# Loading the first two tiles of a row-maximum kernel side by side, from two queues, at the first instruction

## The chip, the cores and the metric

The kernel runs on one core of one Trainium2 chip. The metric is the device time of one execution in microseconds (us), lower is better. The profile's own span is some 1.8 us shorter than the device time (626.4 us of the 628.2 us of the profiled run before), so spans are compared with spans and times with times.

## The reference

```python
def reference(x):                                  # x: 8192 x 8192 float32
    return np.linalg.norm(x, ord=np.inf, axis=1)   # per row: the largest |x|
```

All 268.4 MB have to be read once; the result is 32 KB.

## The kernel before

Three quarters of the rows are the bulk: 24 tiles of 128 partitions x 16384 values, two rows in each partition, 64 KB per partition and 8.39 MB per tile. SyncE's queue loads them into three rotating buffers, and VectorE takes the absolute maximum of each row. The last quarter is cut into ever smaller loads, so that little is left to do after the last byte.

```python
    sbuf = ctx.enter_context(tc.tile_pool(name="sbuf", bufs=BUFS))    # BUFS = 3
    ...
    for a in range(A):                    # A = 6
        for n in range(G):                # G = 4
            t = sbuf.tile([P, W + PAD], F32, tag="t")
            nc.sync.dma_start(out=t[:, :W], in_=x_b[a, n])
            absmax(
                r_bulk[:, a, n * B : (n + 1) * B],
                t[:, :W].rearrange("p (b c) -> p b c", b=B),
            )
    nc.scalar.dma_start(out=out_b, in_=r_bulk[:])
    # ... the last quarter: smaller loads, all from SyncE's queue ...
    nc.at_finalize(start_first_load_early)
    nc.at_finalize(finish_on_pool)
```

`start_first_load_early` is already a start-up optimisation: it moves SyncE's first load ahead of everything else in SyncE's program, so that it is issued before the barrier with which the engines begin.

## Time and profile before

| | before |
|---|---|
| time, median of 3 runs | 628.01 us (627.74 to 628.76) |
| span of the profiled run | 626.4 us |
| the 16 DMA engines | full from 1 us on, 433 GB/s in the steady part |
| VectorE | busy 552.9 us, 88% |
| one tile | transfer 19.35 us, reduce 17.22 us |

The table says that the transfer is the bound: a reduce is 2.1 us shorter than a transfer, so VectorE waits for each tile, and a microsecond that the DMA engines lose is a microsecond of the result. I call a "round" what the 16 DMA engines do in 2.42 us, namely one 64 KB packet each (a packet is the piece of a load that one engine moves at a time). A bulk tile is 8 rounds.

### The profile page before, as it was taken

The page shows a single profiled execution, that of the slowest core. Times are in us where ns is not written, and L with a number is a line of the kernel's source. Part 1 is how long each engine was busy: PE and PEld are TensorE (multiplying, and loading weights), DVE is VectorE, ACT ScalarE, POOL GpSimd, SP SyncE. Part 2 cuts the span into 40 slices and gives each one's busy share as a digit, 9 for nine tenths or more (in the row PEclk, how much of TensorE's full clock was granted, in tenths as well). Part 3 has the DMA queues.
Part 4 walks back from the last instruction along what each step waited for, and adds up shares of the span by engine and source line. Part 5 has one row for each costly group of instructions (what it writes and reads, how often), then busy time and mean ns, then how long its engine had stood idle before and what let it go on. Part 6 is the DMA issues. An engine that isn't in the chain of part 4 may idle for free.

```text
span 626.4 us, 204 instructions
## 1 busy us (share of the span) xinstructions
DVE 552.9 (88%) x67; POOL 0.2 (0%) x4
## 2 busy tenths in 40 slices
DVE  0588988889988889888898888988889999999998
POOL 0000000000000000000000000000000000000000
DMA  9999999999999999999999999999999999999997
GB/s 402 469 402 452 418 452 418 448 423 402 469 402 469 402 469 402 469 402 469 402 469 402 465 406 452 418 452 418 452 404 426 438 428 425 439 423 431 426 422 311
DMA packets 9282, 268.49 MB, mean 429 GB/s; under 512 B 1856, under 2 KB 1856, under 8 KB 3392
## 3 DMA queue, kind: packets, MB, share of 16 engines
q1 hardware_dynamic: 8496, 268.45, 99.4%
q10 hardware_dynamic: 784, 0.02, 0.1%
q14 instruction: 2, 0.02, 0.0%
HBM read 268.44 MB, written 0.03 MB: 429 GB/s over the span
## 4 chain that ended last, share of the span: by engine, by line
DMA 63%; DVE 35%; issue 1%; another core or an unknown queue 0%; DVEq 0%
DMA t<-in_x_dram 63%; DVE r_bulk L140 24%; DVE part L140 8%; DVE t L140 3%; DVEq L220 0%; DVE r_tail L140 0%
## 5 line engine op out<-in xcount | busy, mean ns | idle before, releaser
L140 DVE TENSOR_REDUCE r_bulk<-t 128x2 f32<-128x16384 f32 x24 | 413.3, 17220 | 70.0 <-DMA t<-in_x_dram 70.0
L140 DVE TENSOR_REDUCE part<-t 128x1 f32<-128x8192 f32 (+20 forms) x28 | 121.6, 4410 | 0.9 <-DMA t<-in_x_dram 0.8
L140 DVE TENSOR_REDUCE t<-t 128x1 f32<-128x1664 f32 (+8 forms) x11 | 16.5, 1572 | 0.0
L140 DVE TENSOR_REDUCE r_tail<-t 128x1 f32<-128x644 f32 (+1 forms) x2 | 1.5, 814 | 0.0
L137 DVE MEMSET part<- 128x56 f32 x1 | 0.1, 105 | 0.9 <-PEq L209 0.9
L140 DVE TENSOR_REDUCE r_tail<-part 128x14 f32<-128x56 f32 x1 | 0.2, 211 | 0.0
L209 POOL MEMSET const-bfloat16-1.0<- 128x1 bf16 x1 | 0.1, 101 | 0.0
L209 POOL MEMSET const-uint8-127<- 128x1 uint8 x1 | 0.1, 101 | 0.0
L209 POOL MEMSET const-float32-0.0<- 128x1 f32 x1 | 0.1, 98 | 0.2 <-issue 0.2
L209 POOL MEMSET const-float32-1.0<- 128x1 f32 x1 | 0.1, 98 | 0.0
## 6 DMA issues: line engine op xcount, KB each, us to landing
t<-in_x_dram SPq DMA_DIRECT2D x2, 3392.0 KB, 37.3
t<-in_x_dram SPq DMA_DIRECT2D x1, 5376.0 KB, 40.6
t<-in_x_dram SPq DMA_DIRECT2D x1, 4864.0 KB, 32.9
t<-in_x_dram SPq DMA_DIRECT2D x1, 4800.0 KB, 33.0
t<-in_x_dram SPq DMA_DIRECT2D x1, 4672.0 KB, 34.9
t<-in_x_dram SPq DMA_DIRECT2D x3, 1536.0 KB, 28.7
t<-in_x_dram SPq DMA_DIRECT2D x1, 3520.0 KB, 42.9
t<-in_x_dram SPq DMA_DIRECT2D x1, 3328.0 KB, 40.4
```

What stands on the lines that cost most here:

```text
L137: nc.vector.memset(part[:], 0.0)
L140: nc.vector.reduce_max(out=o, in_=i, axis=X, apply_absolute_value=True)
L209: nc = _bacc.Bacc("TRN2", target_bir_lowering=False, num_devices=1)
```

## The change

The intent is to have the second tile's load in flight from the start too, on a queue of its own. Tile 2's load goes to ScalarE's queue, and both first loads are moved to the head of their engines' programs.

```diff
-def start_first_load_early(nc):
-    sp = mybir.EngineType.SP
+def start_first_loads_early(nc):
     first, *rest = nc.main_func.blocks
-    for block in rest:
-        ...                # the first DMA of SP, moved to the head of the program
+    for engine in (mybir.EngineType.SP, mybir.EngineType.Activation):
+        block, load = next(
+            (b, i)
+            for b in rest
+            for i in b.instructions
+            if i.engine == engine and type(i).__name__ == "InstDMACopy"
+        )
+        assert not load.sync_info.on_wait
+        ...                # moved to the head of that engine's program
@@
-            nc.sync.dma_start(out=t[:, :W], in_=x_b[a, n])
+            queue = nc.scalar if a * G + n == 1 else nc.sync
+            queue.dma_start(out=t[:, :W], in_=x_b[a, n])
```

More of the change, by code (lines that the diff above doesn't have):

```diff
@@ L45, in segments @@
     return out
-def start_first_load_early(nc):
-    sp = mybir.EngineType.SP
+def start_first_loads_early(nc):
     first, *rest = nc.main_func.blocks
-    for block in rest:
-        insts = block.instructions
-        for i, ins in enumerate(insts):
-            if ins.engine == sp and type(ins).__name__ == "InstDMACopy":
-                assert not ins.sync_info.on_wait
-                moved = insts[i]
-                block.instructions = insts[:i] + insts[i + 1 :]
-                head = first.instructions
-                at = next(k for k, h in enumerate(head) if h.engine == sp)
-                first.instructions = head[:at] + [moved] + head[at:]
-                return
+    for engine in (mybir.EngineType.SP, mybir.EngineType.Activation):
[6 more added lines that the diff above has]
+        assert not load.sync_info.on_wait
+        block.instructions = [i for i in block.instructions if i.name != load.name]
+        head = first.instructions
+        at = next(k for k, h in enumerate(head) if h.engine == engine)
+        first.instructions = head[:at] + [load] + head[at:]
 def finish_on_pool(nc):
@@ L192 @@
     nc.sync.dma_start(out=out_t, in_=r_tail[:])
-    nc.at_finalize(start_first_load_early)
+    nc.at_finalize(start_first_loads_early)
     nc.at_finalize(finish_on_pool)
```

## The prediction

> **What bounds the kernel now.** I read the page first, then windows over the first microseconds, then the order of time, then the store at the end of the bulk part. The change only concerns the start, so the question is whether any DMA time is lost there. These are whole lines of the page: the busy tenths in 40 slices, the load queue, and the costliest group.
>
> ```profile
> DVE  0588988889988889888898888988889999999998
> ...
> DMA  9999999999999999999999999999999999999997
> ...
> q1 hardware_dynamic: 8496, 268.45, 99.4%
> ...
> L140 DVE TENSOR_REDUCE r_bulk<-t 128x2 f32<-128x16384 f32 x24 | 413.3, 17220 | 70.0 <-DMA t<-in_x_dram 70.0
> ```
>
> The DMA engines are full in every slice but the last; packets of the one load queue fill 99.4% of the 16 engines' time. VectorE is idle only ahead of the 24 bulk reduces, 70.0 us in all, and always because of a load. The bound is the transfer of 268.4 MB. Windows of the start, and one long window of the steady part (length, busy times, clock, DMA share, GB/s):
>
> ```profile
> 0.00:0.90 0.90, 0.03 (x1) 0.20 (x4) 1.00 0.00 0
> 0.90:1.70 0.80, 0.07 (x1) 0.00 (x0) 1.00 3.80 1311
> 1.70:3.80 2.10, 0.00 (x0) 0.00 (x0) 1.00 0.00 0
> 3.80:4.80 1.00, 0.00 (x0) 0.00 (x0) 1.00 2.42 1049
> ...
> 100.00:400.00 300.00, 267.96 (x16) 0.00 (x0) 1.00 1.00 433
> ```
>
> A packet is booked whole in the window in which it starts. 0.80 us x 1311 GB/s is 1.05 MB, which is 16 packets of 64 KB, one for each engine: the first round of packets starts between 0.9 and 1.7 us, so the load issued at 0.0 needs about 1.0 us to its first byte. The next round starts between 3.8 and 4.8 us, some 3.0 us after the first. In the steady part a round of 1.05 MB takes 1.0486 MB / 433 GB/s = 2.42 us. So the start costs 1.0 us of empty engines and 0.6 us of a slow first round; I see nothing else lost. A tile of 8.39 MB is 8 rounds, 19.35 us. The order of time:
>
> ```profile
> 0.00 58.80 SPq L145 DMA_DIRECT2D t<-in_x_dram  x5
> ...
> 21.95 17.22 DVE L140 TENSOR_REDUCE r_bulk<-t 128x2 f32<-128x16384 f32 x1 [20.98 <-DMA t<-in_x_dram]
> 41.22 17.22 DVE L140 TENSOR_REDUCE r_bulk<-t 128x2 f32<-128x16384 f32 x1 [2.05 <-DMA t<-in_x_dram]
> 60.59 17.22 DVE L140 TENSOR_REDUCE r_bulk<-t 128x2 f32<-128x16384 f32 x1 [2.14 <-DMA t<-in_x_dram]
> ```
>
> Tiles land at about 21.9, 41.2 and 60.6 us, 19.3 us apart: one tile's transfer time with no gap. Between 0 and 2 us the same view counts three load issues on SyncE's queue (at 0.00, 0.79 and 1.17 us), so the second load waits in the queue from about 1 us on, and its turn comes only some 20 us later. Issuing it 0.8 us sooner brings nothing by itself.
>
> **What the Trainium skill says.** "DMA: Bandwidth & Descriptors", section "Issuing engines are not separate DMA queues": transfers started by different engines end on the same 16 DMA engines and interleave, and several issuers only save the sequencers' issue time. Section "Queues, rings and completion order" of that page: each DMA engine goes round between the queues that have work, packet by packet. The trace of before agrees with both, because one transfer of it, the bulk result's store, comes from ScalarE's queue while loads run (the page's lines, then the DMA view of the window 487.8 to 543):
>
> ```profile
> q10 hardware_dynamic: 784, 0.02, 0.1%
> ...
> out_dram<-r_bulk ACTq DMA_DIRECT2D x1, 24.0 KB, 59.1
> ```
> ```profile
> DMA packets 1580, 24.00 MB, mean 435 GB/s; under 512 B 864, under 2 KB 864, under 8 KB 864
> ...
> q1 hardware_dynamic: 796, 23.97, 100.5%
> q10 hardware_dynamic: 784, 0.02, 0.8%
> ```
>
> A store of 24 KB took 59.1 us, since its 784 packets went one for one with 796 load packets. And the rate during this alternation is 435 GB/s against 433 alone: changing queues costs nothing that shows. The page's section "Where 436 GB/s comes from" puts the ceiling of the 16 ports at 435 GB/s; the measured 433 is already there, so a second queue has no idle bandwidth to take. "Perfetto Trace Analysis", section "DMA Instruction — HWDGE (DVE, Sync)", says that an issuing sequencer locks the descriptor generator for itself; no run here shows yet two issues at once, but if it holds the second issue waits some 0.4 us (an issue lasts 0.33 to 0.61 us here), not more.
>
> **The change part by part.** It removes one SyncE issue (0.33 us, not on the path: the engines have 20 us of work by then). It adds one issue on ScalarE, which does nothing else until 484 us. ScalarE and SyncE then reach the opening barrier perhaps 0.4 us later; this delays VectorE's small memset and the third load's issue (now at about 1.2 us), neither of which is needed before 20 us. Cost on the path: 0.
>
> What does move is the order of bytes. Tile 1 (SyncE) and tile 2 (ScalarE) now alternate. With strict turns tile 1 gets the odd rounds, 1 to 15, and tile 2 the even ones, 2 to 16; tile 3, behind tile 1 in SyncE's queue, gets 17 to 24. Tile 1 lands 7 rounds later than now, 21.95 + 7 x 2.42 = 38.9 us; tile 2 at 41.2 and tile 3 at 60.6 us as now. The first reduce starts at 38.9 instead of 21.95 us, so VectorE is 17 us late. (The alternation may start later: the store was issued at 484.2 us, and all its packets lie after 487.8, so a queue that is ahead may keep its lead for a few packets. With four rounds of lead tile 1 lands on round 12, at 31.6 us; tile 3 then starts to take turns with the rest of tile 2, which lands on round 19, at 48.6 us. VectorE is then late by a similar amount.)
>
> Does the lateness reach the loads? A load waits for the reduce that frees its buffer (three buffers). With one reduce each 17.24 us from 38.9, reduces end and the next loads are issued at 56.1 (load 4), 73.4 (load 5) and 90.6 us (load 6), instead of 39.2, 58.5 and 77.8. The engines need them when the load before is through: at about 60, 79.9 and 99.3 us. The slack is 4, 6.5 and 8.7 us, growing by 19.35 - 17.24 = 2.1 us per tile, and a fresh issue needs 1.0 us to its first byte. So the queue never runs dry. VectorE makes up 17 us at 2.1 us per tile within about 8 tiles; from about 180 us on, everything is where it was. Its total agrees: 38.9 + 24 x 17.24 = 452.7 us, less than the 467 us at which the last bulk reduce starts now.
>
> The end is then untouched: the last loads land near 623 us as now, followed by the same short reduce and store. Sum: 0 on the start, 0 in the rate, 0 at the end, so 628.0 us.
>
> **The rivals.**
> First, a gain: two queues could fill part of the 1.0 us before the first byte or the slow first round. For it: that is the only empty DMA time in the trace. Against it: the first load is already the first instruction, ScalarE starts no sooner, and one packet per engine is enough to keep the engine occupied. The most it can give is 1.0 + 0.6 = 1.6 us, 626.4 us; I expect at most a few tenths.
>
> Second, VectorE's lateness becomes a new wait. If both tiles end together at 41.2 us (for instance if ScalarE's packets go first, since the reduces run in program order), load 4 is issued at 58.5 and has its first byte at 59.5 us, when the first engines have just run out. A bubble of up to 1 us would then stay to the end, since the DMA bound never gives time back: 629 us. For it: the slack there is about nothing. Against it: SyncE's issue comes first in the trace by some 0.1 us, and later loads have several us.
>
> Third, large packets from two queues might not interleave freely: if each change of queue cost what the first round did, 15 changes x 0.6 us would be 9 us, 637 us. Against it: 435 GB/s in the store's window, though the store's packets are tiny. Even this is within 2%.
>
> Fourth, there is no alternation of 64 KB packets at all, and tile 1 goes wholly first: then the trace stays as it is, 628.0 us.
>
> **Range and chances.** The main line and the fourth rival give 628.0; the first pulls down to 626.4 at most, the second up to 629. Runs of the kernel before alone spread from 627.74 to 628.76. I choose 628.0 with 626.9 to 629.1. Two per cent is 12.6 us, and no mechanism above reaches it: faster 0.01, within 2% 0.98, slower 0.01.
>
> **What would show each step right or wrong.** Right: VectorE's first reduce starts between 31 and 41 us and its idle time before it nearly doubles; the next eight or so reduces run with no idle time between them; total idle before the bulk reduces stays near 70 us; the window 100 to 400 us shows 433 GB/s; loads 4 to 6 are issued some 17 us later; the page's DMA line stays at 9 in all slices. If the first reduce stays at 22 us, the fourth rival holds. A window between 56 and 64 us under 433 GB/s would be the second rival's bubble; a lower rate between 1 and 41 us the third. The prediction is wrong if the first round starts clearly before 0.9 us, if two queues together exceed 433 GB/s, or if loads are issued late beyond the first three.

## The result

| | before | after |
|---|---|---|
| time, median of 6 runs | 627.96 us (627.74 to 628.76) | 631.16 us (630.74 to 631.53) |
| span of the profiled run | 626.4 us | 629.5 us |
| ratio | 1 | 1.0049, 95% interval 1.0036 to 1.0062 |

Ratios here are the mean time of one kernel's fast runs over that of the other's of the same rounds, so they are not quite the ratio of the medians quoted. The change costs 3.2 us. That is half a per cent, but well outside the scatter. The page of the changed kernel, the same lines as before plus the second queue's:

```profile
DVE  0039999999988898888998888988889999999998
...
DMA  9999999999999999999999999999999999999996
...
q1 hardware_dynamic: 8352, 260.06, 96.0%
q10 hardware_dynamic: 928, 8.41, 3.2%
...
L140 DVE TENSOR_REDUCE r_bulk<-t 128x2 f32<-128x16384 f32 x24 | 412.6, 17217 | 74.1 <-DMA t<-in_x_dram 74.1
```

VectorE now starts in the third slice of 15.7 us rather than the second, then works without idle slices, and is back in step by slice 12. Its total idle time ahead of the bulk reduces went from 70.0 to 74.1 us, so it is not slower; something it waits for came later. At 40 slices the DMA line hides what happened. The order of time shows the start (start, length, engine, what; in brackets the idle time before and its end):

```profile
0.00 198.19 SPq L147 DMA_DIRECT2D t<-in_x_dram  x11
0.12 0.39 ACTq L147 DMA_DIRECT2D t<-in_x_dram  x1
...
41.90 137.10 DVE L140 TENSOR_REDUCE r_bulk<-t 128x2 f32<-128x16384 f32 x8 [40.78 <-DMA t<-in_x_dram]
180.61 17.22 DVE L140 TENSOR_REDUCE r_bulk<-t 128x2 f32<-128x16384 f32 x1 [1.61 <-DMA t<-in_x_dram]
```

Tile 1 lands at 41.9 us, not at 21.9. Eight reduces follow without a gap, and before the reduce at 180.6 us VectorE waits for a load again. Load 4 was issued at 39.2 us in the kernel before (first line: SyncE's queue from 30 us on, load 4 and the eight after it); in the changed kernel the view of that queue between 56 and 62 us has it as its one entry:

```profile
39.20 155.37 SPq L145 DMA_DIRECT2D t<-in_x_dram  x9
```
```profile
59.15 0.33 SPq L147 DMA_DIRECT2D t<-in_x_dram  x1
```

And this is what the DMA engines did around that moment. Windows of the kernel before, then of the changed kernel (length, busy times, clock, DMA share, GB/s):

```profile
41.00:58.00 17.00, 16.78 (x1) 0.00 (x0) 1.00 1.00 432
58.00:68.00 10.00, 7.86 (x2) 0.00 (x0) 1.00 0.97 419
```
```profile
41.00:58.00 17.00, 16.10 (x1) 0.00 (x0) 1.00 1.04 451
58.00:68.00 10.00, 10.00 (x2) 0.00 (x0) 1.00 0.90 341
...
100.00:400.00 300.00, 275.19 (x17) 0.00 (x0) 1.00 1.00 435
```

A window counts a packet whole where it starts, so a short one can stand some per cent off (419 for 433). But 341 GB/s against 419 over 10 us is 0.78 MB, or 1.8 us at 433 GB/s, averaged over the 16 engines. The steady rate afterwards is the same (435 and 433), so nothing is lost or regained there.

The single packet records of both traces give the account engine by engine (they do not name the engine; I follow each one by its next packet starting where the last ended). The end of a round on the slowest of the 16 engines:

| end of round, slowest engine | before | after | difference |
|---|---|---|---|
| 9 | 24.00 | 23.94 | -0.1 |
| 10 | 26.41 | 27.04 | +0.6 |
| 24 (end of load 3) | 60.25 | 60.85 | +0.6 |
| 26 (two rounds into load 4) | 65.09 | 69.09 | +4.0 |
| 192 (end of the bulk) | 466.56 | 470.12 | +3.6 |
| last landing | 623.61 | 626.67 | +3.1 |

Of the loss, 0.6 us arises in round 10 (a round of 3.0 us in the middle of the first two tiles) and 3.4 us at the change from load 3 to load 4. Most of it then stays to the end: the difference falls by 0.4 us up to the end of the bulk, where the kernel before has some slow rounds of its own, and by 0.5 us in the last quarter. The fastest engine lost only 1.8 us by round 26 (64.35 and 66.11 us), so the engines are spread by 3.0 us in the changed kernel and by 0.7 in the kernel before. A load is complete when its slowest engine is (load 4's sixteenth and last completion came at 83.94 us, and at 79.94 in the kernel before, again 4.0 us apart), hence the slowest counts.

### The profile page after: what moved, and what is told of

It is laid out like the page before. It is cut to its first block, busy times and chain, and to the rows that moved or that the text cites. A ratio compares the mean times of both kernels' runs of the same rounds, so it can differ in the third digit from the quotient of the medians.

```text
span 629.5 us, 204 instructions
## 1 busy us (share of the span) xinstructions
DVE 552.2 (88%) x67; POOL 0.2 (0%) x4
## 4 chain that ended last, share of the span: by engine, by line
DMA 50%; DVE 48%; issue 1%; DVEq 0%
DMA t<-in_x_dram 50%; DVE r_bulk L140 32%; DVE part L140 14%; DVE t L140 3%; DVEq L222 0%; DVE r_tail L140 0%
## 5 line engine op out<-in xcount | busy, mean ns | idle before, releaser
L140 DVE TENSOR_REDUCE r_bulk<-t 128x2 f32<-128x16384 f32 x24 | 412.6, 17217 | 74.1 <-DMA t<-in_x_dram 74.1
```

What stands on the lines that cost most here:

```text
L140: nc.vector.reduce_max(out=o, in_=i, axis=X, apply_absolute_value=True)
```

## The experiments

Theory A: the two queues alternate, so tile 1 lands only together with tile 2, at 41.9 us; its reduce frees the buffer for load 4 at 59.15 us, when the engines are about to run dry. Rival B: the second queue slows the transfers themselves, or leaves a disorder behind. Rival C: the earlier second issue, or the opening barrier that ends later for it, costs the time. Each run below was timed in five rounds beside the kernel before on the same chip. All results passed the comparison with the reference, even that of the run which leaves out values.

### The early issue without the second queue

```diff
-    for engine in (mybir.EngineType.SP, mybir.EngineType.Activation):
+    for engine in (mybir.EngineType.SP, mybir.EngineType.SP):
@@
-            queue = nc.scalar if a * G + n == 1 else nc.sync
-            queue.dma_start(out=t[:, :W], in_=x_b[a, n])
+            nc.sync.dma_start(out=t[:, :W], in_=x_b[a, n])
```

(The insertion point is also moved behind a load that already stands there, so that tile 1 stays first.)

> Both first loads at the program's first instruction, but both from SyncE's queue. Theory A (two queues alternate, tile 1 lands only with tile 2 at 41.9 us, load 4 is issued at 59.15 us when the engines run dry): here nothing alternates, tile 1 lands at 21.9, load 4 is issued at 39.2, time 628.0, ratio to before 1.000. Rival C (the early second issue or the later barrier costs the 3 us): 631.1, ratio 1.005.

Measured: 627.80 us, before 627.86, ratio 1.0002 (0.9989 to 1.0014). The first reduce starts at 21.99 us. Issuing both loads early from one queue neither helps nor harms; rival C falls.

### The second queue without the early issue

```diff
-    for engine in (mybir.EngineType.SP, mybir.EngineType.Activation):
+    for engine in (mybir.EngineType.SP,):
```

> Tile 2 from ScalarE's queue, but issued where the program has it, after the opening barrier (some 0.7 us), not at the first instruction. Theory A: the first round lasts until 3.9 us, so the queues alternate all the same: first reduce at 41.9, load 4 at 59.1, 631.1, ratio 1.005. Rival C (the early issue costs it): 628.0. The slow tenth round (3.0 us in place of 2.42) should show again if it belongs to the second queue.

Measured: 627.95 us, before 627.86, ratio 1.0001 (0.9987 to 1.0015). I had expected 631, so this run surprised me, and it says the most. Its order of time, then SyncE's queue between 56 and 62 us, then a window:

```profile
0.79 0.39 ACTq L147 DMA_DIRECT2D t<-in_x_dram  x1
...
39.10 85.72 DVE L140 TENSOR_REDUCE r_bulk<-t 128x2 f32<-128x16384 f32 x5 [38.13 <-DMA t<-in_x_dram]
```
```profile
56.35 0.33 SPq L147 DMA_DIRECT2D t<-in_x_dram  x1
```
```profile
58.00:68.00 10.00, 10.00 (x1) 0.00 (x0) 1.00 1.02 433
```

The queues do alternate here. But the packet records show SyncE's queue served in rounds 1 and 2 before ScalarE's first packet in round 3, whereas in the changed kernel round 2 is already ScalarE's. With that lead of one round tile 1 has its last data in round 14, and lands at 39.1 us instead of 41.9. Load 4 is issued at 56.35 us, 3.4 us ahead of the first engine's end of load 3 (59.78), and nothing is lost. So two queues and a VectorE that is 17 us late do not lose time by themselves; what differs is that load 4 is issued 2.8 us earlier, and that no round 10 is slow. Rival B falls too, as far as the alternation is concerned.

### The changed kernel with a shorter first reduce

```diff
+            v = t[:, :W].rearrange("p (b c) -> p b c", b=B)
+            if a * G + n == 0:
+                v = v[:, :, : cols // 2]
-            absmax(r_bulk[:, a, n * B : (n + 1) * B], t[:, :W].rearrange("p (b c) -> p b c", b=B))
+            absmax(r_bulk[:, a, n * B : (n + 1) * B], v)
```

> The changed kernel with the first reduce over the first half of the columns of tile 1's rows only (wrong result on purpose, it takes 8.6 us in place of 17.2): load 4 is issued at about 50.6, 9 us before the engines need it, with two queues as before. Theory A: the gap at 60 us goes, about 2.5 us of the 3.1 come back, 628.6 (0.6 left, the slow tenth round), ratio 1.001. Rival B (the second queue slows the transfers themselves, or the skew it leaves does): 631, ratio 1.005.

Measured: 628.15 us, before 627.86, ratio 1.0004 (0.9992 to 1.0017). Tile 1 lands at 41.9 us as in the changed kernel, but load 4 is issued at 50.63 us (first line). The window that showed the loss is full (second line):

```profile
50.63 0.33 SPq L147 DMA_DIRECT2D t<-in_x_dram  x1
```
```profile
58.00:68.00 10.00, 10.00 (x2) 0.00 (x0) 1.00 1.01 439
```

The two queues, the early issue, the late landing and VectorE's late start are all still there; only the buffer comes free earlier, and by the two ratios 2.8 of the 3.2 us are gone (1.0049 - 1.0004 = 0.0045, times 628 us). This is the direct test of theory A. Round 10 is slow here too (2.72 us; lengths of rounds are medians of the 16 engines), and yet no loss can be told from zero at the end; the kernel before has a slow spell of its own of about 0.4 us, between rounds 30 and 70 by the packet records, which this one does not have.

### The late load 4 without a second queue

In the kernel before, extra reduces of tile 1 hold its buffer, so that load 4 is issued late from the single queue. A first attempt:

```diff
+    scratch = outp.tile([P, 1], F32)
@@
+            if a * G + n == 0:
+                for w in (16384, 1800):
+                    absmax(scratch[:], t[:, :w])
```

> The kernel before, one queue, with two extra reduces of tile 1 (16384 and 1800 columns) behind the first, into a scratch column: load 4 is issued at about 58.5 us, as late against the end of load 3 as in the changed kernel (that is 0.6 us further on there). Theory A: the same gap without a second queue, about 2.5 us, 630.5, ratio 1.004. Rival B: 628.0.

Measured: 643.41 us, before 627.86, ratio 1.0248 (1.0234 to 1.0262). The aim was missed. Both extra reduces write the same scratch column, and the program that was built has the second one behind tile 2's reduce. The order of time, then windows:

```profile
39.15 17.21 DVE L141 TENSOR_REDUCE scratch<-t 128x1 f32<-128x16384 f32 x1
56.28 17.21 DVE L141 TENSOR_REDUCE r_bulk<-t 128x2 f32<-128x16384 f32 x1
73.41 2.02 DVE L141 TENSOR_REDUCE scratch<-t 128x1 f32<-128x1800 f32 x1
```
```profile
60.00:74.00 14.00, 14.00 (x2) 0.00 (x0) 1.00 0.00 0
```

Load 4 went out at 73.52 us, 14.0 us after the first engine had ended load 3 (59.50), and the run lost 15.6 us. So here the lateness is paid in full, plus about 1.5 us for the restart. With a scratch column for each extra reduce the order held, and three runs set load 4 where I wanted it:

```diff
+    scratch = outp.tile([P, 2], F32)
@@
+            if a * G + n == 0:
+                for k, w in enumerate((16384, 2056)):
+                    absmax(scratch[:, k : k + 1], t[:, :w])
```

> One queue, the kernel before, two extra reduces of tile 1 (16384 and 2056 columns) into two scratch columns, so that nothing orders them otherwise: load 4 is issued at about 58.5 us, 1 us ahead of the first engine's end of load 3, as in the changed kernel. Theory A (the late load 4 costs the 3 us, with or without a second queue): the slowest engine loses about 2.9 us, 630.8, ratio 1.0047. Rival B (it takes two queues to lose it): 627.9.

> The same with one extra reduce of 16384 columns: load 4 is issued at about 56.35 us, 3.2 us ahead of the end of load 3, as in the run with the later ScalarE issue, which lost nothing. Theory A: 627.9, ratio 1.000, VectorE's 17 us being absorbed by about tile 10. If lateness of VectorE as such costs time: over 629.

> The same with extra reduces of 16384 and 3976 columns: load 4 is issued at about 60.5 us, at the end of load 3. Theory A: every further microsecond of lateness is paid in full, so 2.0 us more than with 58.5, or a little less if the late start of the first packets there is not repeated: 631.5 to 632.8, ratio 1.006 to 1.008.

After these a fourth, with 16384 and 1060 columns:

> One queue, the kernel before with extra reduces of 16384 and 1060 columns behind the first: load 4 is issued at about 57.6 us, between 56.35 (which lost nothing) and 58.65 (which lost 2.8 us), 1.9 us ahead of the first engine's end of load 3. A fresh load needs 1.0 to 1.7 us to its first packets on idle engines, so if that lead is all that counts the loss is under 0.5 us: 628.2. If descriptors that come while the engines still run arrive as late as they did with 58.65 (up to 3.6 us after the issue), it loses 1 to 2 us: 629 to 630.

All in one table, by the lead of the issue over the first engine's end of load 3. The last column is the ratio to the kernel before, with its interval:

| run | queues | load 4 issued | lead | time | before | ratio |
|---|---|---|---|---|---|---|
| later ScalarE issue | 2 | 56.35 | 3.4 | 627.95 | 627.86 | 1.0001 (0.9987 to 1.0015) |
| one extra reduce | 1 | 56.53 | 3.1 | 628.09 | 627.77 | 1.0003 (0.9990 to 1.0017) |
| 1060 columns more | 1 | 57.46 | 2.0 | 628.41 | 628.22 | 1.0004 (0.9992 to 1.0017) |
| 2056 columns more | 1 | 58.65 | 0.9 | 630.56 | 627.77 | 1.0045 (1.0033 to 1.0058) |
| the changed kernel | 2 | 59.15 | 0.7 | 631.16 | 627.96 | 1.0049 (1.0036 to 1.0062) |
| 3976 columns more | 1 | 60.67 | -1.2 | 630.32 | 627.77 | 1.0039 (1.0027 to 1.0052) |
| the first attempt | 1 | 73.52 | -14.0 | 643.41 | 627.86 | 1.0248 (1.0234 to 1.0262) |

The run with 2056 columns repeats the changed kernel's loss with a single queue: 2.8 us at about the same lead. Its window from 58 to 68 us has the bubble too:

```profile
58.00:68.00 10.00, 10.00 (x2) 0.00 (x0) 1.00 0.82 295
```

A lead of 2 us or more costs nothing that these runs can tell from zero, though at 2.0 us the slowest engine already ended the first round of load 4 1.0 us later than in the kernel before (63.69 and 62.67 us). My expectation for 60.5 us was wrong: an issue 2.0 us later does not cost 2.0 us more but, if anything, a little less. The packet records show the difference. With the issue at 60.67 us all engines were idle, and their first packets of load 4 start between 61.62 and 62.29 us, 0.95 to 1.62 us after it. With the issue at 58.65 us the engines were on their last packets of load 3; load 4 starts between 59.81 and 62.23 us, up to 3.6 us after the issue, and its first two rounds take 3.2 and 3.1 us, where the run with idle engines has one of 3.0 us and then 2.42. The changed kernel has the same picture (60.12 to 62.68 us, rounds of 3.3 and 2.7 us). Counted from the issue to the slowest engine's end of its first round, that is 4.7 us with idle engines, but 7.0 us with the issue at 58.65 and 7.5 in the changed kernel. (At the start of the kernel, where the engines are idle as well, it is 4.6 to 4.9 us in all the runs above, though the last of the 16 first packets starts anywhere from 1.6 to 2.5 us.) The order of time around these two issues:

```profile
58.65 17.45 SPq L146 DMA_DIRECT2D t<-in_x_dram  x2
```
```profile
60.67 17.46 SPq L146 DMA_DIRECT2D t<-in_x_dram  x2
```

Why the packets of a load that is issued during the last packets of the load before start so unevenly, no run here shows.

### Who takes turns with whom

```diff
-            queue.dma_start(out=t[:, :W], in_=x_b[a, n])
+            if a * G + n == 1:
+                for lo in range(0, W, cols):
+                    queue.dma_start(out=t[:, lo : lo + cols], in_=x_b[a, n][:, lo : lo + cols])
+            else:
+                queue.dma_start(out=t[:, :W], in_=x_b[a, n])
```

> The changed kernel with tile 2 in two loads of half a row pair each, both from ScalarE's queue, so that its packets are 32 KB and SyncE's 64 KB. If the queues take turns packet by packet, tile 1 is through after 8 x (64 + 32) KB per engine, 12 rounds, and lands at about 31.6 us; load 4 is issued at 48.9, in time. The rest of tile 2 then takes turns with tile 3 and lands at about 61 us; its reduce ends at about 78.4 and load 5 is issued some 1 us ahead of the end of load 4: the gap moves to load 5, about 630.5, ratio 1.004. If the queues share by bytes, tile 1 lands at 41.5 as in the changed kernel and load 4 is late: 631.

Measured: 648.45 us, before 627.77, ratio 1.0328 (1.0314 to 1.0342). As a test of the time it failed: the first reduce in the trace waits for tile 2's two loads and only the second one waits for tile 1's, since the program was built with tile 2's reduce first. So the first reduce began only at 61.2 us:

```profile
61.21 17.22 DVE L140 TENSOR_REDUCE r_bulk<-t 128x2 f32<-128x16384 f32 x1 [60.10 <-DMA t<-in_x_dram]
```

Load 4 was issued at 78.46 us, and the engines stood idle meanwhile. As a test of the turns it succeeded: tile 1's sixteenth completion came at 31.95 us and tile 2's second half at 61.12, where I had expected 31.6 and 61 for turns packet by packet, and 41.5 for shares by bytes.

The completions themselves take a turn as well. The DMA view of two windows of the changed kernel, 38.1 to 40.5 us and 40.55 to 41.6 us (queue, packets, MB, share of the engines):

```profile
q10 hardware_dynamic: 16, 1.05, 100.8%
```
```profile
DMA packets 48, 1.05 MB, mean 999 GB/s; under 512 B 32, under 2 KB 32, under 8 KB 32
...
q1 hardware_dynamic: 32, 1.05, 231.1%
q10 hardware_dynamic: 16, 0.00, 0.9%
```

In the first window only ScalarE's queue starts packets, the 16 with tile 2's last data. In the second come 32 packets under 512 B, one on each queue and engine, and SyncE's 16 packets of tile 3. The packet records give their sizes and order: on each engine, tile 1's last data ends (38.2 to 39.1 us), then tile 2's last data passes, then a packet of 4 B on SyncE's queue, then one on ScalarE's. Tile 1's completions, the counts that VectorE waits for, arrive with the former, from 40.90 to 41.88 us. Its data was there 2.8 us before VectorE was told. In the kernel before, where the 4 B packets follow the data at once, it is 0.35 us (21.58 and 21.93 us). The run with tile 2 in halves tests this: there the packet of ScalarE's queue that passes first has 32 KB and takes 1.21 us instead of 2.42, and the delay is 1.5 us (30.41 and 31.95), 1.2 us shorter.

### Side by side within one tile

```diff
-            queue = nc.scalar if a * G + n == 1 else nc.sync
-            queue.dma_start(out=t[:, :W], in_=x_b[a, n])
+            if a * G + n == 0:
+                for queue, lo in ((nc.sync, 0), (nc.scalar, cols)):
+                    queue.dma_start(out=t[:, lo : lo + cols], in_=x_b[a, n][:, lo : lo + cols])
+            else:
+                nc.sync.dma_start(out=t[:, :W], in_=x_b[a, n])
```

> Two queues side by side at the first instruction, but on the two halves of tile 1, with tile 2 behind on SyncE's queue. Theory A: the two loads alternate and end together, but together they are one tile, so tile 1 lands at about 22 us as in the kernel before, load 4 is issued at about 39.3, 627.9, ratio 1.000; a gain is not expected, since the first bytes come no earlier than 1.0 us. If two queues at the start are harmful as such: 630 or more. If they fill the slow first round: 627.2.

Measured: 627.73 us, before 628.22, ratio 0.9994 (0.9980 to 1.0008). The order of time:

```profile
22.07 17.22 DVE L140 TENSOR_REDUCE r_bulk<-t 128x2 f32<-128x16384 f32 x1 [20.94 <-DMA t<-in_x_dram]
```

Two queues at the first instruction are harmless when what lands together is one tile. The interval holds 1, so a gain over the kernel before is not shown. No run found a version that beats it.

## Why the prediction was wrong

**The bound, the start and the turns** were right. The first round again started at 1.0 us; the two issues at the first instruction cost the barrier 0.15 us and the result nothing, as the run with both on one queue shows. The queues took strict turns, and the rate while they did was not lower but for one round.

**Tile 1's landing** was the first step that failed. The text put it at 38.9 us, one round ahead of tile 2, by counting data packets. It left out that the completion is a packet of its own which waits for a turn behind tile 2's last one. Measured: 41.9 us. Its last data had ended at 38.2 to 39.1 us, so the count of the data rounds was right but for the slow round 10.

**The slack of load 4** followed from that. "At 56.1 ... the slack is 4" became 59.15 us and 0.7 us. The later loads did have several us, as written, and VectorE was back in step at 180 us, as written.

**The second rival** had the right mechanism, though not for the reason that it named (ScalarE's packets going first): both tiles end together, load 4 is issued near 58.5 us, and a bubble stays to the end. I gave it too little weight and too small a size, because I reckoned with a fixed 1.0 us from the issue to the first byte. At this lead the first packets started 1.0 to 3.5 us after the issue, with two slow rounds behind them, and the slowest engine lost 3.4 us (1.8 on average of the 16). The run with one queue at a lead of 0.9 us shows the same loss, and the one with the short first reduce takes it away.

**The other rivals.** The gain was not there. A cost for each change of queue did not show: all rounds but one of the first two tiles took 2.42 us after the start. That one, round 10, cost 0.6 us at that point. It is in two of the three profiles that have the two queues side by side at the first instruction on two tiles (the third, with tile 2 in halves, has a few slow packets near 17.5 and 32.5 us instead), and not in the one with the later ScalarE issue. The run with both loads on one queue has a single slow packet at that time (2.91 us in round 9). The cause of round 10, and whether the slow round counts at all in the end, stay open.

**The range** of 626.9 to 629.1 us missed 631.2. The chance of 0.98 for a change within 2% rested on no mechanism reaching 12.6 us, and held. One reading was slightly off without consequence: VectorE of the kernel before is also idle for 0.9 us ahead of later reduces, not only ahead of the 24 of the bulk.

## What to carry to other kernels

Here two equal loads issued side by side, on DMA engines that one queue already kept full, did not come sooner; both came when the later one would have, so the consumer started late and the first buffers came free late. Before splitting loads over queues, work out when the next load can be issued against the moment the queue runs dry, and leave 2 to 3 us: with that much lead no loss could be told from zero here, with 0.7 to 0.9 us about 3 us were. If both queues are wanted, give the load that is needed first a head start of one packet, or put both on halves of the same tile: both were harmless here, and neither was faster than one queue.

## What the Trainium skill lacked or had wrong

- "DMA: Bandwidth & Descriptors", section "Queues, rings and completion order", describes turns between queues by packet, and that a completion lands only after the earlier writes of its engine. It does not say that the completion itself takes a turn, so that a data packet of another queue can pass between it and its own data: tile 1's came as a 4 B packet behind the other queue's 64 KB, 2.8 us after its last data (39.1 and 41.9 us).
- The same page, section "Issuing engines are not separate DMA queues", says that several issuers only save the sequencers' time. It leaves out the price: two equal loads side by side both land at the end (41.9 us, where one queue had 21.9 and 41.2), which cost 3.2 us here.
- The same page, section "Latency and other measured facts", gives about 600 ns to the first byte for these queues. Here the first packets start 1.0 to 1.65 us after the issue at the start of the kernel before (up to 2.5 us in the run with one extra reduce), 0.95 to 1.62 us in the run with load 4 at 60.67, and up to 3.6 us when the issue falls into the last packets of the load before. No page has the last.
- "Perfetto Trace Analysis", section "DMA Instruction — HWDGE (DVE, Sync)", says that an issue locks the descriptor generator for itself. Two issues that overlapped (from 0.00 and 0.12 us) lasted 0.38 and 0.39 us (SyncE's lasts 0.38 us alone too, in the kernel before), and two that began together at 0.79 us, in the run with the later ScalarE issue, 0.33 and 0.39 us. Had one of these waited for the other, it would have lasted some 0.7 us (an estimate, the sum of the two): no waiting shows.
- No page says that the 16 engines keep a spread once they have it: 3.0 us between the fastest and the slowest in round 26, and 2.8 at the end of the bulk 400 us later (467.31 and 470.12).
